# Layer 0 of a two-layer diffusion backbone: six output blocks kept split, early first weights, low parts of the norms on VectorE

## The chip, the cores and the metric

The kernel runs on one core of one Trainium2 chip. The metric is the device time of one execution in microseconds (us); the time before is the median of three runs. TensorE is the matrix engine, VectorE (DVE in the rows) and ScalarE (ACT) work on elements, POOL is GpSimd, and SP is the queue from which nearly all DMAs are issued.

## The reference, cut to what matters

There are 512 latent tokens and 256 context tokens of width 1024, and two layers. The change lies mostly in layer 0:

```
x, h: 512 latent tokens, 256 context tokens
layer 0:
  y = concat(gated_linear_heads(u), windowed_attention(u)) @ w_out      # mixer
  x = layer_norm(ALPHA * x + gate * y)                                  # first norm
  x = layer_norm(ALPHA * x + gate5 * squared_relu(mod(x) @ w1) @ w2)    # MLP, second norm
  the same for h with its own modulation
layer 1: other mixers, then the same pair of norm and MLP, latent tokens only
```

The modulation vectors (gate, shift, scale) are products of two conditioning vectors with large matrices.

## The kernel before, in words

**Numbers.** Dense products are made in fp32r, a format of fewer bits. Each operand is split in two: a high part, cast by ScalarE, and a low part, which is what the cast left, subtracted by VectorE (`split`, L323 to L326). A product is three matmuls, high x high (L346), high weight x low activation (L348) and low weight x high activation (L350), in that order for each of eight slices k of 128 rows. Activations lie transposed, 128 features by tokens, latents first (512 columns), then context (256).

**Weights** (`weights`, L328). A block of 128 x 1024 is loaded into a raw buffer by a DMA from SP and then split into a high and a low buffer. Without `keep`, the buffers come from the pool `wp`, which rotates them: in layer 0 after the mixer five raw, two high and two low. With `keep` each block has high and low buffers of its own. Load and split are given a priority 1000 places ahead of their place in the code (`prio`, PW). The framework turns the code into one ordered list per engine: what has its operands and buffers ready and the lowest priority number goes next, by a modelled time. On the chip every engine, and SP's queue, runs its list in order, and a tile that takes the place of an older one waits until that one's last reader is done.

**Layer 0's mixer** (`mixer0`). The gated-linear heads (`gla`) and the eight attention heads (`gqa`, scores one head ahead of `attend`) are interleaved as generators; when `gla` has ended, attention runs on alone. A head ends with two logarithms and an exponential on ScalarE (L832 to L834), two products on VectorE (L839, L840), and for every second head the split of the result into activation slice 4 + h/2 (L325, L326). The pool `m1` holds the gated-linear part's work tiles, `mb` those of attention; `m0` what both need.

**Output projection** (`project`). For two token parts (512 latent, 256 context columns), for eight output blocks d: get weight block d, 24 matmuls into one of six PSUM banks, add to the residual z (L1032), add z up for the norm (L1034, L1036). Layer 0 keeps no block: the eight blocks are loaded and split for the latents and again for the context. After a part, the generator `norm` of that part becomes `fill`, and two of its steps are taken after each block of the next part.

**Norm** (`norm`). Mean by a matmul with ones (L1066), subtraction on VectorE (L1076), squares on ScalarE (L1078), their mean by matmuls (L1074), reciprocal root on ScalarE (L1085, L1086). Then for each k: product on VectorE (L1090), the high part of the next activation on ScalarE (L1103), the same unrounded on VectorE into `lnu` (L1104), and their difference, the low part, on POOL (L1106). ScalarE then scales z (L1112). This happens twice in layer 0 for both parts (512 and 256 columns) and once in layer 1 for two halves of 256.

**MLP** (`mlp`). Four hidden blocks at a time. For the first four, `first` goes over the parts; on the latents the blocks are taken in the pairs (0, 1) and (2, 3), with one step of the context part's norm after every second k; on the context one by one. `up` and `down` follow for the rest. Between them `step` takes a row of the modulation matrices of later use (`ada_chunk`): it is loaded into a raw buffer of the same five and reduced by VectorE (L394).

Of the kernel before, what the change touches and what calls it, by code (L numbers as in the profile page):

```python
# [16 lines left out]
P = 128  # L17
D = 1024
KT = D // P
# [25 lines left out]
PL = 50  # L45
PZL = 300
# [189 lines left out]
def blocks(*ws):  # L236

    return [tuple(w[d].rearrange("p k m -> p (k m)") for w in ws) for d in range(KT)]
# [21 lines left out]
class Build:  # L260
# [67 lines left out]
    def weights(self, src, n=1024, keep=None, lead=PW):  # L328

        raw = self.wp.tile([P, 1024], F32, tag="wraw", name="wraw")  # L330
        pool, bufs, d = (self.wp, 2, '') if keep is None else (keep[0], 1, keep[1])
        hi = pool.tile([P, 1024], F32R, tag=f"whi{d}", name="whi", bufs=bufs)
        lo = pool.tile([P, 1024], F32R, tag=f"wlo{d}", name="wlo", bufs=bufs)
        with self.prio(-lead):
            src = src if isinstance(src, tuple) else (src,)
            m = n // len(src)
            for i, s in enumerate(src):
                self.nc.sync.dma_start(raw[:, i * m:i * m + m], s)
            self.split(raw[:, :n], hi[:, :n], lo[:, :n])
        return hi[:, :n], lo[:, :n]  # L340
# [372 lines left out]
    def gqa(self, m0, mx_, queries, KS, K2, vg, hi, lo):  # L713
# [73 lines left out]
        def attend(h):  # L787
# [41 lines left out]
            mm(oc[:, 0:256], sl, Q2[sink, CX], start=False, stop=True)  # L829
            r, ro = HALF[par], HALF[1 - par]  # L830
# [21 lines left out]
        for h in range(8):  # L852
            a = scores(h + 1) if h < 7 else iter(())
            for _ in attend(h):
                next(a, None)
                yield
            for _ in a:
                yield

    def mixer0(self):  # L860
# [3 lines left out]
        with tc.tile_pool(name="m0", bufs=1, side="right", reuse_waits="tile") as m0, ExitStack() as m0_, \  # L864
# [119 lines left out]
            with tc.tile_pool(name="mb", bufs=1, reuse_waits="tile") as mb:  # L984
                self.zerob = mb.tile([P, P], BF16, name="zerob")
                nc.gpsimd.memset(self.zerob, 0.0)
                self.identb = mb.tile([P, P], BF16, name="identb")
                nc.gpsimd.tensor_copy(self.identb, ident)
                self.maskb = [mb.tile([P, P], BF16, name=f"maskb{i}") for i in range(2)]
                mt = m1.tile([P, 2 * P], F32, tag="Dt", name="mt", bufs=4)  # L990
                nc.sync.dma_start(mt, self.a['band'])
                for i in range(2):
                    nc.gpsimd.tensor_copy(self.maskb[i], mt[:, i * P:(i + 1) * P])
                self.gla_setup(mb)

# [12 lines left out]
                for _ in att:  # L1008
                    pass
            self.psum(**PF)  # L1010
        return mhi, mlo


    def project(self, ws, hi, lo, z, g, l, parts, sums, norm, keep=None, kept=(), lead=PW):
# [6 lines left out]
        for i, (t0, m) in enumerate(parts):  # L1021
            sl = slice(t0, t0 + m)
            for d in range(KT):
                wh, wl = kept.get(d) or self.weights(ws[d], keep=keep and (keep, d), lead=lead)
                if keep:
                    kept[d] = wh, wl
# [21 lines left out]
    def norm(self, pool, z, sums, l, i, w, part, act=None, nxt=None, out=None, spill=None):  # L1048
# [39 lines left out]
        for k in range(KT):  # L1088
# [12 lines left out]
            else:  # L1101
# [3 lines left out]
                eng = nc.gpsimd  # L1105
                eng.tensor_tensor(lo[:, k, sl], u, hi[:, k, sl].bitcast(F32), op=ALU.subtract)  # L1106
# [11 lines left out]
    def mlp(self, pool, l, hi, lo, z, parts, fill, step=lambda: None, first_parts=None):  # L1118
# [14 lines left out]
        def first():  # L1133
# [3 lines left out]
            for i, (t0, m) in enumerate(first_parts or parts):  # L1137
                sl = slice(t0, t0 + m)
                for pair in ((0, 1), (2, 3)) if i == 0 else ((0,), (1,), (2,), (3,)):
# [51 lines left out]
    def layer0(self):  # L1191
        nc, tc = self.nc, self.tc
        hi, lo = self.mixer0()
        self.wopen(5)
        self.fq = self.es2.enter_context(tc.tile_pool(name="fq", bufs=1, side="right", reuse_waits="tile"))
        fq = self.fq
        with tc.tile_pool(name="zp", bufs=1, side="right", reuse_waits="tile") as zp, \
# [25 lines left out]
            fill = self.project(blocks(self.a['w0_o']), ks(hi), ks(lo), z, 2, 0, PARTS, sums, norm(0, (0, 4, 3)))  # L1223
            hs = self.mlp(f0, 0, *act, z, PARTS, fill, step)
            for _ in gen:
                pass
            fill = self.project(blocks(self.a['w2_0'][6], self.a['w2_0'][7]), *hs, z, 5, 0, PARTS, sums, norm(1, (1, 1, 0), self.zd))

            self.shift_setup(fq)
# [7 lines left out]
            for _ in fill:  # L1237
                pass
        return act
# [778 lines left out]
    def wopen(self, bufs=3):  # L2018
# [42 lines left out]
```

## Time and profile before

| | us |
|---|---|
| three runs | 2063.58, 2064.16, 2066.43 |
| median | 2064.16 |
| profiled execution, its own time | 2064.74 |
| its span, first to last instruction | 2063.0 |

The median is what the comparison goes by; the rows are of the profiled execution. In a row of the timeline the first number is the start in us from the span's beginning, the second the time until the group's last end; [x <-y] is the idle time of the engine just before it, and what ended it. PE is TensorE's matmul stream, PEld its weight loads. Matmul rows overlap, so their starts say more than their lengths.

### The profile page before, as it was taken

What the parts mean: (1) busy time and instruction counts of PE and PEld (TensorE: products, weight loads), DVE (VectorE), ACT (ScalarE), POOL (GpSimd) and SP (SyncE); (2) the same over time, 40 slices, a digit from 0 to 9 for tenths busy, and PEclk for the clock granted to TensorE, in tenths of its full rate; (3) what the DMA queues carried; (4) which work ended last, traced back from release to release, by engine and by line L of the source; (5) the groups of instructions that cost most, each with busy time, mean ns of one, the idle gap of its engine ahead of it and who ended that gap; (6) DMA issues with size and microseconds to landing.
All of it is one profiled execution on the core that took longest, in us unless ns stands there. A gap on an engine that the chain in (4) does not pass through costs nothing.

```text
span 2063.0 us, 35320 instructions
## 1 busy us (share of the span) xinstructions
PE 1937.1 (94%) x14244; PEld 1613.2 (78%) x14244; DVE 1311.3 (64%) x2341; ACT 962.4 (47%) x1840; POOL 295.9 (14%) x503
## 2 busy tenths in 40 slices
PE   8999798999999999999989999988888999999998
PEld 7887666677788888888877876757776888888887
DVE  8785999638897556534485455467876665444454
ACT  5536777535522222222255656766665654333332
POOL 0003566202100000000021020024231020000001
PEclk9998899999999999999999999998999999999999
DMA  8650000053454555313243100000001513323241
GB/s 297 213 167 11 1 1 1 1 204 112 132 167 134 156 163 148 112 53 92 82 140 139 47 1 19 16 8 3 3 3 34 167 42 94 108 92 91 89 137 42
DMA packets 67047, 181.67 MB, mean 88 GB/s; under 512 B 7490, under 2 KB 12354, under 8 KB 66756
## 3 DMA queue, kind: packets, MB, share of 16 engines
q1 hardware_dynamic: 66884, 179.42, 27.9%
q8 instruction: 112, 1.84, 0.4%
q14 instruction: 51, 0.42, 0.1%
HBM read 172.83 MB, written 5.51 MB: 86 GB/s over the span
## 4 chain that ended last, share of the span: by engine, by line
PE 68%; DVE 15%; ACT 8%; DMA 4%; issue 4%; POOL 1%; SPq 0%; DVEq 0%; ACTq 0%; POOLq 0%
PE mm L350 17%; PE mm L348 17%; PE mm L346 17%; DMA araw<-in_ada_r_dram 3%; PE var L1074 2%; DVE wlo L326 2%; PE mo L1492 1%; PE ms L1466 1%; PE gab L1624 1%; DVE aprod L394 1%; PE gx L1740 1%; DVE z L1090 1%; DVE lq L621 1%; DVE araw L394 1%; PE go L795 1%
## 5 line engine op out<-in xcount | busy, mean ns | idle before, releaser
L325 ACT CAST whi<-wraw 128x1024 fp32r<-128x1024 f32 (+2 forms) x253 | 221.8, 880 | 625.6 <-PE mm L348 538.2
L346 PE MATMUL mm<-acthi,whi 128*128 128x512 f32 (+1 forms) x1464 | 446.2, 351 | 10.8 <-ACT whi L325 10.1
L350 PE MATMUL mm<-acthi,wlo 128*128 128x512 f32 (+1 forms) x1464 | 440.4, 347 | 9.2 <-DVE wlo L326 9.2
L348 PE MATMUL mm<-actlo,whi 128*128 128x512 f32 (+1 forms) x1464 | 442.7, 348 | 1.6 <-POOL actlo L1106 1.5
L326 DVE TENSOR_TENSOR wlo<-wraw,whi 128x1024 fp32r<-128x1024 f32 (+2 forms) x253 | 258.3, 1024 | 207.0 <-ACT whi L325 200.5
L346 PEld LDWEIGHTS mm<-acthi,whi 128*128 128x128 f32 x1464 | 252.1, 192 | 49.5 <-ACT whi L325 12.5
L350 PEld LDWEIGHTS mm<-acthi,wlo 128*128 128x128 f32 x1464 | 252.0, 192 | 48.7 <-DVE wlo L326 12.8
L348 PEld LDWEIGHTS mm<-actlo,whi 128*128 128x128 f32 x1464 | 252.3, 192 | 40.6 <-issue 3.9
L350 PE MATMUL mm<-hh,wlo 128*128 128x512 f32 (+1 forms) x832 | 253.1, 342 | 3.6 <-DVE wlo L326 3.6
L346 PE MATMUL mm<-hh,whi 128*128 128x512 f32 (+1 forms) x832 | 255.2, 344 | 0.2 <-ACT hh L325 0.2
L348 PE MATMUL mm<-hl,whi 128*128 128x512 f32 (+1 forms) x832 | 253.2, 342 | 0.1
L1106 POOL TENSOR_TENSOR actlo<-lnu,acthi 128x256 fp32r<-128x256 f32 (+1 forms) x48 | 59.9, 1263 | 715.2 <-DVE lnu L1104 635.2
L350 PEld LDWEIGHTS mm<-hh,wlo 128*128 128x128 f32 x832 | 143.5, 189 | 23.5 <-DVE wlo L326 4.2
L348 PEld LDWEIGHTS mm<-hl,whi 128*128 128x128 f32 x832 | 144.0, 189 | 20.2 <-issue 0.7
L346 PEld LDWEIGHTS mm<-hh,whi 128*128 128x128 f32 x832 | 143.3, 189 | 19.9 <-issue 1.0
L1178 DVE SCALAR_TENSOR_TENSOR z<-mm,mod,z 128x512 f32<-128x512 f32 (+1 forms) x144 | 94.1, 660 | 98.3 <-PE mm L350 98.1
L394 DVE SCALAR_TENSOR_TENSOR araw<-araw,scb 128x1024 f32<-128x1024 f32 x80 | 97.9, 1223 | 54.8 <-DMA araw<-in_ada_r_dram 53.9
L325 ACT CAST hh<-relu 128x512 fp32r<-128x512 f32 (+1 forms) x100 | 50.6, 535 | 79.7 <-DVE relu L1130 79.7
L1032 DVE SCALAR_TENSOR_TENSOR z<-mm,mod,z 128x256 f32<-128x256 f32 (+1 forms) x64 | 35.0, 549 | 76.7 <-PE mm L350 75.7
L619 POOL TENSOR_TENSOR lk<-kd,Dt 64x128 f32<-64x128 f32 x144 | 75.5, 524 | 35.0 <-ACT Dt L601 13.5
L326 DVE TENSOR_TENSOR hl<-relu,hh 128x512 fp32r<-128x512 f32 (+1 forms) x100 | 56.2, 588 | 26.5 <-ACT hh L325 26.2
L394 DVE SCALAR_TENSOR_TENSOR aprod<-araw,scb 128x1024 bf16<-128x1024 f32 x48 | 58.6, 1222 | 22.1 <-DMA araw<-in_ada_r_dram 21.8
(462 smaller groups left out, 3215.3 us busy)
## 6 DMA issues: line engine op xcount, KB each, us to landing
araw<-in_ada_r_dram SPq DMA_DIRECT2D x80, 512.0 KB, 3.8
wraw<-in_w_dram SPq DMA_DIRECT2D x72, 512.0 KB, 3.6
wraw<-in_w_dram SPq DMA_DIRECT2D x144, 256.0 KB, 2.7
wraw<-in_w_s_dram SPq DMA_DIRECT2D x31, 512.0 KB, 4.0
wraw<-in_w_o_dram SPq DMA_DIRECT2D x22, 512.0 KB, 3.6
scraw<-in_ada_sc_dram SPq DMA_DIRECT2D x8, 512.0 KB, 7.5
shraw<-in_ada_sh_dram SPq DMA_DIRECT2D x8, 512.0 KB, 6.1
x<-in_xT_dram SPq DMA_DIRECT2D x8, 384.0 KB, 5.6
```

The costliest lines, as they stand in the source:

```text
L325: self.nc.scalar.copy(hi, raw)
L326: (eng or self.nc.vector).tensor_tensor(lo, raw, hi.bitcast(F32), op=ALU.subtract)
L346: mm(o, whi, ahi[:, sl], start=first, stop=False)
L348: mm(o, whi, alo[:, sl], start=False, stop=False)
L350: mm(o, wlo, ahi[:, sl], start=False, stop=last)
L394: self.nc.vector.scalar_tensor_tensor(pr, raw, 1.0, self.scb[:, w], op0=ALU.mult, op1=ALU.mult, accum_out=out(w))
L619: nc.gpsimd.tensor_tensor(K[r, :, x], kk[r, :, x], d[r, :, x], op=ALU.mult)
L621: nc.vector.tensor_tensor(Q[r, :, y], qq[r, :, y], d[r, :, y], op=ALU.mult)
L1032: nc.vector.scalar_tensor_tensor(zs, o, self.mod[:, l, self.wh(i, parts), g, d:d + 1], zs, op0=ALU.mult, op1=ALU.add)
L1074: nc.tensor.matmul(var, self.c('o1024', 0, P), sq, start=(k == 0), stop=(k == KT - 1))
L1106: eng.tensor_tensor(lo[:, k, sl], u, hi[:, k, sl].bitcast(F32), op=ALU.subtract)
L1178: nc.vector.scalar_tensor_tensor(z[:, d, sl], o, self.mod[:, l, self.wh(i, parts), 5, d:d + 1], z[:, d, sl], op0=ALU.mult, op1=ALU.add)
```

## The change

It has six parts. Six blocks (`KO`, d = 2 to 7) of layer 0's output projection are kept split, in a pool `fk` whose place the MLP's hidden tiles (`fh`) and then the tiles of the shift (`fs`) take over later. The pool of weights is opened inside the mixer, when the last head has only its closing elementwise work left and `m1` has been closed, and blocks 0 and 1 are asked for there (`first`). That pool has four raw, three high and two low buffers instead of five, two and two. The low parts in `norm` go from POOL to VectorE, in all norms that feed another product. The second pair of the MLP's first latent part becomes two single blocks in layer 0. The zero, identity and mask tiles of attention come after the clearing of the second set of level tiles in the code, at a priority 100 places ahead.

```diff
-        hi = pool.tile([P, 1024], F32R, tag=f"whi{d}", name="whi", bufs=bufs)
+        hi = pool.tile([P, 1024], F32R, tag=f"whi{d}", name="whi", bufs=bufs if keep else self.wb)
...
             mm(oc[:, 0:256], sl, Q2[sink, CX], start=False, stop=True)
+            if h == 7:
+                yield True
...
-            for _ in attend(h):
+            for last in attend(h):
                 next(a, None)
-                yield
+                yield last
...
-                self.zerob = mb.tile([P, P], BF16, name="zerob")
-                nc.gpsimd.memset(self.zerob, 0.0)
...
                 self.gla_setup(mb)
+                with self.prio(-100):
+                    self.zerob = mb.tile([P, P], BF16, name="zerob")
+                    nc.gpsimd.memset(self.zerob, 0.0)
...
-                for _ in att:
-                    pass
+                for last in att:
+                    if last:
+                        break
+            m0_.close()
+            self.wopen(4, 3)
+            ws = blocks(self.a['w0_o'])
+            first = {d: self.weights(ws[d]) for d in range(2)}
+            for _ in att:
+                pass
             self.psum(**PF)
-        return mhi, mlo
+        return mhi, mlo, first
...
-                wh, wl = kept.get(d) or self.weights(ws[d], keep=keep and (keep, d), lead=lead)
-                if keep:
+                k = keep and d in keeps
+                wh, wl = kept.get(d) or first.pop(d, None) or self.weights(ws[d], keep=k and (keep, d) or None, lead=lead)
+                if k:
                     kept[d] = wh, wl
...
-                eng = nc.gpsimd
-                eng.tensor_tensor(lo[:, k, sl], u, hi[:, k, sl].bitcast(F32), op=ALU.subtract)
+                nc.vector.tensor_tensor(lo[:, k, sl], u, hi[:, k, sl].bitcast(F32), op=ALU.subtract)
...
-                for pair in ((0, 1), (2, 3)) if i == 0 else ((0,), (1,), (2,), (3,)):
+                for pair in ((0, 1), (2,), (3,)) if i == 0 and l == 0 else ((0, 1), (2, 3)) if i == 0 else ((0,), (1,), (2,), (3,)):
...
-        hi, lo = self.mixer0()
-        self.wopen(5)
+        hi, lo, first = self.mixer0()
...
-            fill = self.project(blocks(self.a['w0_o']), ks(hi), ks(lo), z, 2, 0, PARTS, sums, norm(0, (0, 4, 3)))
-            hs = self.mlp(f0, 0, *act, z, PARTS, fill, step)
+            with tc.tile_pool(name="fk", bufs=1, reuse_waits="tile") as fk:
+                fill = self.project(blocks(self.a['w0_o']), ks(hi), ks(lo), z, 2, 0, PARTS, sums, norm(0, (0, 4, 3)), fk,
+                                    first=first, keeps=KO)
+            fh_ = ExitStack()
+            fh = fh_.enter_context(tc.tile_pool(name="fh", bufs=1, reuse_waits="tile"))
+            hs = self.mlp(fh, 0, *act, z, PARTS, fill, step)
...
+            fh_.close()
+
+            fs_ = ExitStack()
+            f0 = fs_.enter_context(tc.tile_pool(name="fs", bufs=1, reuse_waits="tile"))
```

## Rows read from the trace of the kernel before

**Rows 1.** The page, part 1: busy time, share of the span, instructions.

```profile
PE 1937.1 (94%) x14244; PEld 1613.2 (78%) x14244; DVE 1311.3 (64%) x2341; ACT 962.4 (47%) x1840; POOL 295.9 (14%) x503
```

**Rows 2.** Windows: length; busy PE, PEld, DVE, ACT, POOL; PEclk; DMA share; GB/s.

```profile
400.00:420.00 20.00, 18.92 (x76) 11.83 (x75) 4.94 (x14) 9.58 (x19) 0.21 (x4) 0.83 0.08 26
420.00:430.00 10.00, 4.98 (x12) 3.45 (x13) 5.24 (x18) 4.04 (x6) 0.00 (x0) 0.74 0.82 290
```

**Rows 3.** Timeline 415 to 432: start, us, engine, line, operation [idle before, releaser].

```profile
415.44 12.19 SPq L338 DMA_DIRECT2D wraw<-in_w_o_dram  x7
...
419.93 0.38 PE L829 MATMUL goc<-q,sel 3*128 3x256 f32 x1
...
422.35 0.93 ACT L325 CAST acthi<-ga 128x512 fp32r<-128x512 f32 x2 [0.76 <-DVE ga L839]
...
424.27 0.50 PE L346 MATMUL mm<-acthi,whi 128*128 128x512 f32 x1 [3.97 <-ACT whi L325]
...
426.19 0.80 PE L350 MATMUL mm<-acthi,wlo 128*128 128x512 f32 x1 [1.05 <-DVE wlo L326]
...
431.48 0.43 PE L350 MATMUL mm<-acthi,wlo 128*128 128x512 f32 x1
```

**Rows 4.** Timeline of ScalarE: two neighbouring high-part casts of the output projection.

```profile
460.99 1.06 ACT L325 CAST whi<-wraw 128x1024 fp32r<-128x1024 f32 x1 [4.38 <-PE mm L348]
...
466.43 1.06 ACT L325 CAST whi<-wraw 128x1024 fp32r<-128x1024 f32 x1 [4.38 <-PE mm L348]
```

**Rows 5.** Timeline of TensorE, from the projection's context part to the MLP's steady part.

```profile
471.89 0.28 PE L346 MATMUL mm<-acthi,whi 128*128 128x256 f32 x1
...
474.76 1.02 PE L1066 MATMUL mu<-sums,col 128*128 128x512 f32 x2
...
478.49 1.88 PE L1074 MATMUL var<-lnsq,col 128*128 128x512 f32 x4
...
496.62 0.58 PE L350 MATMUL mm<-acthi,wlo 128*128 128x256 f32 x1 [2.16 <-DVE wlo L326]
...
555.44 0.52 PE L346 MATMUL mm<-acthi,whi 128*128 128x512 f32 x2
```

**Rows 6.** Window, latent norm's second half: length; busy DVE; PEclk; DMA share; GB/s.

```profile
489.90:518.00 28.10, 28.10 (x36) 0.94 0.30 96
```

**Rows 7.** Timeline of VectorE, and POOL's first row, in the same stretch.

```profile
424.92 2.36 DVE L326 TENSOR_TENSOR wlo<-wraw,whi 128x1024 fp32r<-128x1024 f32 x2
...
491.12 0.54 DVE L1104 TENSOR_SCALAR lnu<-z,gb 128x512 f32<-128x512 f32 x1
...
491.83 1.30 POOL L1106 TENSOR_TENSOR actlo<-lnu,acthi 128x512 fp32r<-128x512 f32 x1 [73.95 <-DVE lnu L1104]
...
491.96 1.44 DVE L1104 TENSOR_SCALAR lnu<-z,gb 128x512 f32<-128x512 f32 x1
...
526.86 1.29 DVE L326 TENSOR_TENSOR hl<-relu,hh 128x512 fp32r<-128x512 f32 x2
```

**Rows 8.** Timeline of TensorE in layer 0's second norm: first, fifth and last gap.

```profile
1064.05 0.38 PE L350 MATMUL mm<-hh,wlo 128*128 128x256 f32 x1 [2.16 <-DVE wlo L326]
...
1081.35 0.50 PE L348 MATMUL mm<-actlo,whi 128*128 128x512 f32 x1 [0.89 <-POOL actlo L1106]
...
1106.70 0.50 PE L350 MATMUL mm<-acthi,wlo 128*128 128x512 f32 x1 [0.65 <-DVE wlo L326]
```

**Rows 9.** Timeline of SP's queue and TensorE in the MLP's steady part.

```profile
736.64 0.33 SPq L408 DMA_DIRECT2D araw<-in_ada_r_dram  x1
...
741.59 0.33 SPq L408 DMA_DIRECT2D araw<-in_ada_r_dram  x1
...
758.90 0.62 PE L350 MATMUL mm<-acthi,wlo 128*128 128x512 f32 x2 [0.20 <-DVE wlo L326]
```

**Rows 10.** Timeline of POOL and TensorE at the start of the GLA stage.

```profile
203.17 0.21 POOL L986 MEMSET zerob<- 128x128 bf16 x1
...
205.15 0.28 PE L645 MATMUL base<-zerob 128*128 128x256 bf16 x1
```

More of the change, by code (lines that the diff above doesn't have):

```diff
@@ L45 @@
 PL = 50
+KO = 2, 3, 4, 5, 6, 7
 PZL = 300
@@ L984, in mixer0 @@
             with tc.tile_pool(name="mb", bufs=1, reuse_waits="tile") as mb:
-                self.zerob = mb.tile([P, P], BF16, name="zerob")
-                nc.gpsimd.memset(self.zerob, 0.0)
[L987 to L993, printed above, removed]
-                self.gla_setup(mb)
+                self.gla_setup(mb)
+                with self.prio(-100):
+                    self.zerob = mb.tile([P, P], BF16, name="zerob")
+                    nc.gpsimd.memset(self.zerob, 0.0)
+                    self.identb = mb.tile([P, P], BF16, name="identb")
+                    nc.gpsimd.tensor_copy(self.identb, ident)
+                    self.maskb = [mb.tile([P, P], BF16, name=f"maskb{i}") for i in range(2)]
+                    mt = m1.tile([P, 2 * P], F32, tag="Dt", name="mt", bufs=4)
+                    nc.sync.dma_start(mt, self.a['band'])
+                    for i in range(2):
+                        nc.gpsimd.tensor_copy(self.maskb[i], mt[:, i * P:(i + 1) * P])
                 def queries(i):
@@ L1007, in mixer0, with project @@
                         next(att, None)
-                for _ in att:
-                    pass
+                for last in att:
[7 more added lines that the diff above has]
+                pass
             self.psum(**PF)
-        return mhi, mlo
-    def project(self, ws, hi, lo, z, g, l, parts, sums, norm, keep=None, kept=(), lead=PW):
+        return mhi, mlo, first
+    def project(self, ws, hi, lo, z, g, l, parts, sums, norm, keep=None, kept=(), lead=PW, first={},
+                keeps=range(KT)):
         nc = self.nc
@@ L1238, in layer0 @@
                 pass
+            fs_.close()
         return act
@@ L2016, in close, with wopen @@
         self.es.close()
-    def wopen(self, bufs=3):
+    def wopen(self, bufs=3, wb=2):
+        self.wb = wb
         self.wes = ExitStack()
```

## The prediction

> **What bounds the kernel now.** I read the page's busy shares first: TensorE is busy 94% of the span and VectorE 64% [rows 1], so the time is TensorE's own work plus the places where TensorE waits. What matters is where those places are. The windows by stage came next [rows 2]. Around the hand-over from layer 0's attention to its output projection TensorE is busy 4.98 of 10 us, at a mean granted clock of 0.74, while ScalarE is about half used in the 20 us before. The timeline of that hand-over [rows 3] shows why. The last attention matmul starts at 419.93 and lasts 0.38; the projection's first matmul starts at 424.27, after 3.97 us of waiting for the first weight block's high part; the third waits again, for the low part, until 426.19. The weight loads are issued from 415.44 on. The thirteen matmuls from 426.19 to 431.48 start 0.44 us apart, the lower of the clock's two levels (1.2 GHz); later a block of 24 takes 5.44 [rows 4], 0.227 apiece, the upper level (2.4 GHz).
>
> Second place: from the first 256-column matmul of the projection (471.89) to the first matmul of the MLP's steady part (555.44) TensorE stops again and again, mostly for a low part made on VectorE, 2.16 us at 496.62 for instance [rows 5]. In that stretch VectorE is busy all of 28.10 us [rows 6]. Third place: the same pattern in the second norm of layer 0, seven gaps from 1064.05 to 1106.70 that make 6.8 us together, one of them behind the low part that POOL writes [rows 8].
>
> **The parts, step by step.**
>
> *Hand-over.* Blocks 0 and 1 are loaded and split before the last head ends, so TensorE can go on at 420.31 (419.93 + 0.38 [rows 3]). Its first 21 matmuls need k = 0 to 6, which exist; k = 7 is written by the casts of 422.35 and the subtractions right behind them, and TensorE gets there at 420.31 + 21 x 0.227 = 425.1. A block takes 5.44 us at the full clock (distance of the casts at 460.99 and 466.43 [rows 4]), eight take 43.5; before, 471.89 - 420.31 = 51.6 [rows 3, 5]. With no idle gap there the clock should not fall. So up to 8.1 us go. Against this, two casts of 1.06 [rows 4] and two subtractions of 1.2 [rows 7] now stand among the last heads' work, and SP's and ScalarE's queues are in order: an exponential behind such a cast is late by up to 1.06 (two: 2.1), by more if the cast has been queued ahead of data that isn't there. VectorE has room (4.94 busy of 20 [rows 2]). Between 0 and 8.1, I take 1.0 of cost: **-7.1 us**. Other loads aren't passed: SP has nothing else to issue there, and the z loads come later, as now, behind the weights; the six PSUM banks of the products cover their lateness.
>
> *Kept blocks, three high buffers, single second pair, low parts on VectorE: 471.89 to 555.44, 83.55 us.* TensorE's own work in it, at the full clock: eight projection blocks of 2.87 (471.89 to 474.76 [rows 5]) make 23.0; four MLP blocks of 24 x 0.23 = 5.5 make 22.0; four of 2.87 make 11.5; the latent norm's sums take 0.9 plus four groups of 1.7 (1.88 less the overlap [rows 5]), the context norm's about half, together 12.3. Sum 68.8, so 14.7 us are lost now. What VectorE had to do in its full 28.10 us [rows 6] shrinks: six blocks are no longer split a second time (6 x 1.2 = 7.2 of VectorE, 6 x 1.06 = 6.4 of ScalarE, and six loads of 512 KB). The low parts cost 8 x 0.62 more (the equal form, 1.29 for two [rows 7]) = 5.0. But POOL's part was not free: beside it lnu took 1.44 instead of 0.54 [rows 7], 0.9 for each of eight, 7.2. Net 28.1 - 7.2 + 5.0 - 7.2 = 18.7, so VectorE ends some 9 us sooner and the MLP's first matmul waits for nothing. With three high parts the next cast doesn't wait for TensorE, and blocks 2 and 3 one by one let the context norm advance 12 steps instead of 8 in the first part, so its results are there when the MLP's 256-column blocks want them. What is late next: the low part of block 2, which has only two buffers and follows the pair (0.3 to 1.2 us), and the context sums (about 1). I leave 3.2 of the 14.7: **-11.5 us**; bounds -5 and -14.7.
>
> What POOL costs VectorE: the row shows 0.9 us lost per POOL subtraction that itself takes 1.30 [rows 7]. The Trainium skill, SBUF — State Buffer, section "Who interferes with whom", says that such a pair excludes each other for the whole instruction. By that each would cost VectorE up to 1.30, and the relief would be 10.4 instead of 7.2; as an estimate, the next part would then gain some 3 us more and the forecast come to 2040.5. The measured 0.9 stands.
>
> *Second norm of layer 0.* No weights are kept here; only POOL's share goes and the third high buffer comes. VectorE: 8 x (0.62 - 0.9) = -2.2 for the latents, about the same again for POOL's own latency, which TensorE waited for at 1081.35 [rows 8]. Of 6.8 us I take **-2.8**; bounds +2 (VectorE no freer) and -6.8. Layer 1's 16 low parts (256 columns): at nothing, 1 us either way, since VectorE pays and is repaid alike.
>
> *Four raw buffers instead of five*, shared by weights and modulation rows during the MLP. There SP issues the next row when the one before has been used, 736.64 and 741.59, and TensorE waits 0.20 us at 758.90 [rows 9]. One buffer less shortens the lead of the weights; the third high part gives back a little. Between 0 and +4: **+0.4**.
>
> *Order of the mask tiles and the clearing in POOL's queue.* The zero tile is written at 203.17, its first reader starts at 205.15 without a wait [rows 10]: 1.8 us of cover, so nothing. If the ten clearings came first, up to 2 us. The pools that now share memory (kept blocks, then the hidden layer, then the shift) follow each other on TensorE: nothing.
>
> Sum: -7.1 - 11.5 - 2.8 + 0.4 = -21.0. The profiled execution took 2064.74 (span 2063.0), 0.6 above the median 2064.16: 2043.7 against it, **2043.5** rounded towards the median.
>
> **Rivals.**
> 1. *The hand-over keeps its wait in another place.* The early buffers lie where the gated-linear part's tiles were; if they come free late, or the casts stand in front of the last heads' exponentials with their data still on the way, the 8.1 us are paid there. For it: ScalarE's order is fixed, attention is a chain over it. Against: ScalarE is half idle [rows 2]. Then 2050.6. Chance 0.10.
> 2. *VectorE becomes the bound.* If the long rows beside POOL are not POOL's doing but something that stays, VectorE's stretch shrinks only from 28.1 to 25.9, the first gain falls to about 5 and the second norm loses 2.5: 2043.5 + 6.5 + 5.3 = 2055.3. Against it: the same forms are short when POOL is quiet [rows 7]. Chance 0.14.
> 3. *Slower: the row chain with four buffers.* One modulation row circulates in 4.95 us (736.64 to 741.59 [rows 9]); a step of the MLP's second half takes 12 x (0.227 + 0.12) = 4.2, so a group of eight falls behind by 8 x 0.79 = 6.3 us, which the weights asked for ahead cover. With one buffer less the lead is 3 x 4.2 = 12.5; the lag and one more circuit want 6.3 + 4.95 = 11.3. If it is a little worse, TensorE waits up to 6.3 in each of the four groups that carry rows: +25, that is 2068.7. It decides where the lead falls under the lag. For it: 0.20 us of waiting already. Chance 0.07.
> 4. *Something in the order changes elsewhere* (GLA stage, layer 1), or the stalls of the second place return in other spots: near 2060. Chance 0.07.
>
> **How the numbers follow.** The forecast has 0.62. About 0.2% (4 us) is what a measurement of this kernel can tell from no change. Forecast and rivals 1 and 2 are all faster by more, 0.86, plus 0.02 of rival 4: 0.88; same 0.05 (rest of rival 4); slower 0.07. Low end: all bounds on the good side give -30.6; 2036 takes most of it. High end: past rival 2, 2057. Outside remain rivals 3 and 4 and the tails, under 0.2.
>
> **What would show it.** Right: the matmul after the last attention matmul follows within 1 us and the projection's first part takes about 44 us at clock 1.00; no POOL row at the norm's low part, lnu 0.54 throughout; sixteen output-projection splits become ten; from the first 256-column matmul to the MLP's steady part about 72 us; gaps of the second norm near 4. Wrong: an exponential of the last heads waiting behind a high-part cast; VectorE still full for 25 us; TensorE waits for low parts between 556 and 860 in groups of eight.

## The result and the profile after

The changed kernel takes 2040.17 us (median of 4 runs, 2037.43 to 2043.07) against 2063.87 for the kernel before in the same comparison: ratio 0.989, 95% interval 0.9872 to 0.9908. The forecast was 2043.5 in a range of 2036 to 2057. The profiled execution took 2037.43 (span 2035.5), 27.3 less than the one before; it is the fastest of the four, so the stages below add up to more than the medians' 23.7. That the total came out near the forecast is in part luck: one term of the sum fell short by 5.2 us and three others brought 12.8 more than forecast.

The timeline of the hand-over after the change, one fence for TensorE, ScalarE, VectorE and SyncE; it answers to [rows 3] and [rows 2]. Columns: start, duration, engine, line, operation, idle time before it and what ended it.

```profile
402.87 28.25 SPq L339 DMA_DIRECT2D wraw<-in_w_o_dram  x9
...
419.42 0.38 PE L830 MATMUL goc<-q,sel 3*128 3x256 f32 x1
423.77 0.50 PE L347 MATMUL mm<-acthi,whi 128*128 128x512 f32 x1 [3.96 <-ACT whi L326]
425.03 0.80 PE L351 MATMUL mm<-acthi,wlo 128*128 128x512 f32 x1 [0.47 <-DVE wlo L327]
...
421.85 0.92 ACT L326 CAST acthi<-ga 128x512 fp32r<-128x512 f32 x2 [0.76 <-DVE ga L842]
422.68 3.88 ACT L326 CAST whi<-wraw 128x1024 fp32r<-128x1024 f32 x4
...
423.75 4.63 DVE L327 TENSOR_TENSOR wlo<-wraw,whi 128x1024 fp32r<-128x1024 f32 x4
```

The first weight load is issued 12.57 us earlier (402.87 for 415.44), the second 5.44 (414.93 for 420.37), and TensorE still waits 3.96 us for the first high part, as before (3.97). ScalarE casts it right behind the last head's closing casts, although the data had lain there for long.

Windows after the change: the hand-over, VectorE's stretch in the first norm, and the second norm with the next stage's input. Columns: stretch, its length, busy time (instructions) of PE, PEld, DVE, ACT, POOL, then the granted clock. The last row is the third window in the kernel before.

```profile
420.00:430.00 10.00, 5.76 (x18) 4.33 (x19) 7.31 (x11) 6.82 (x9) 0.00 (x0) 0.83 0.40 123
487.50:504.60 17.10, 17.10 (x127) 16.37 (x127) 17.10 (x36) 11.96 (x16) 0.00 (x0) 1.00 0.00 1
1034.00:1114.00 80.00, 80.00 (x431) 66.82 (x430) 54.82 (x100) 50.26 (x77) 0.80 (x14) 1.00 0.44 149
```

```profile
1034.00:1114.00 80.00, 73.24 (x382) 59.22 (x380) 63.86 (x94) 46.40 (x69) 22.59 (x26) 0.98 0.40 122
```

VectorE's full stretch shrank from 28.10 us [rows 6] to 17.10, and TensorE is busy through all of it. (The 28.10 also hold two modulation rows of 1.21 us. From the norm's first z to the fourth addition to the context sums VectorE took 25.30 us before, with five splits of weights among them, and 16.68 now, with none.) Over the whole stretch of 83.55 us TensorE's idle time fell from 8.75 us to 0.33 and its busy time from 74.80 to 68.87, at a granted clock of 1.00 instead of 0.94. In the second norm TensorE is busy all of the 80 us, and GpSimd's 22.59 us beside VectorE are gone (the changed kernel is 16 us ahead there, so the two windows don't hold quite the same work). Of the gaps of [rows 5] one of 0.19 us is left in the first norm's stretch, and none of those of [rows 8].

**Where the time went, by stage.** Each stage is the distance of two starts in TensorE's timeline. *Hand-over*: the last head's second value product to the first 256-column block of the projection. *First norm*: from there to the MLP's steady part. *Second norm*: its 256-column part to the end of the next stage's input. *Layer-1 norm*: first mean to the first 512-column block. *RWKV/MLA*: from the second norm's end to the group norm; no experiment edits it, TensorE runs the same matmuls there in the same order in all 14 profiles, and its spread shows what one profile is worth. Medians come from different comparisons, in which the kernel before took 2062.86 to 2067.37; the ratio, taken within each comparison, is what compares.

| kernel | hand-over | first norm | second norm | layer-1 norm | RWKV/MLA | span | median | ratio to before, 95% |
|---|---|---|---|---|---|---|---|---|
| before | 53.02 | 83.55 | 129.47 | 62.83 | 438.67 | 2063.0 | 2063.87 | |
| after | 51.12 | 69.20 | 119.12 | 60.42 | 440.47 | 2035.5 | 2040.17 | 0.989 [0.9872, 0.9908] |
| e1 first weights not early | 51.08 | 69.18 | 118.84 | 60.43 | 440.28 | 2033.1 | 2040.19 | 0.9888 [0.9866, 0.991] |
| e2 no kept blocks | 51.00 | 74.14 | 118.83 | 60.43 | 442.50 | 2042.5 | 2044.67 | 0.9906 [0.9886, 0.9926] |
| e3 low parts on GpSimd | 51.08 | 80.26 | 126.08 | 63.19 | 442.42 | 2058.8 | 2058.75 | 0.9968 [0.9952, 0.9983] |
| e4 two high buffers | 51.05 | 73.04 | 119.30 | 60.40 | 445.04 | 2044.0 | 2045.05 | 0.9902 [0.9881, 0.9923] |
| e5 hidden tiles as before | 52.31 | 72.61 | 119.37 | 60.42 | 440.84 | 2041.1 | 2042.99 | 0.9904 [0.9881, 0.9927] |
| e6 first split on GpSimd | 49.98 | 69.18 | 118.84 | 60.42 | 440.89 | 2035.3 | 2038.23 | 0.9874 [0.9852, 0.9896] |
| e7 layer 1: three high | 52.24 | 69.19 | 118.86 | 58.74 | 441.19 | 2036.3 | 2038.33 | 0.9874 [0.985, 0.9898] |
| e8 before + low parts on VectorE | 52.72 | 75.31 | 119.35 | 60.40 | 439.15 | 2045.3 | 2046.49 | 0.9913 [0.9892, 0.9934] |
| e9 e6 into kept tiles | 45.03 | 69.09 | 119.14 | 60.43 | 443.04 | 2034.5 | 2033.73 | 0.9844 [0.9823, 0.9865] |
| e10 e7, single blocks | 51.08 | 69.20 | 119.15 | 57.22 | 446.34 | 2040.2 | 2040.42 | 0.9868 [0.9846, 0.9889] |
| e11 second pair back | 52.33 | 76.02 | 118.83 | 60.42 | 442.69 | 2045.0 | 2045.39 | 0.99 [0.9874, 0.9926] |
| e12 e9 and e10 | 45.01 | 69.08 | 118.86 | 57.21 | 443.52 | 2036.8 | 2031.27 | 0.9828 [0.9801, 0.9854] |

Before to after: -1.90, -14.35, -10.35, -2.41, and +1.80 in RWKV/MLA; the MLP between the norms took 0.63 more (483.88, 484.51). In RWKV/MLA the longest profiles have the lower granted clock (0.93 in e4, 0.94 in e10, 0.95 in before and after). Still, the two kernels without the change's buffers, before and e8, have the two shortest times of the 14 (438.67, 439.15), so a small cost of the change there isn't excluded.

### The profile page after: what moved, and what is told of

Read it like the earlier page. It is cut to its first block, busy times and chain, and to the rows that moved or that the text cites. A ratio compares the mean times of both kernels' runs of the same rounds, so it can differ in the third digit from the quotient of the medians.

```text
span 2035.5 us, 35292 instructions
## 1 busy us (share of the span) xinstructions
PE 1924.9 (95%) x14244; PEld 1605.9 (79%) x14244; DVE 1301.0 (64%) x2383; ACT 956.2 (47%) x1834; POOL 238.2 (12%) x455
## 4 chain that ended last, share of the span: by engine, by line
PE 74%; DVE 11%; ACT 8%; issue 3%; DMA 3%; POOL 1%; SPq 0%; ACTq 0%; DVEq 0%; POOLq 0%
PE mm L349 18%; PE mm L347 18%; PE mm L351 18%; PE var L1087 2%; DMA araw<-in_ada_r_dram 2%; PE ms L1485 1%; PE mo L1511 1%; PE gab L1643 1%; DVE aprod L395 1%; PE gx L1759 1%; PE go L796 1%; DVE wlo L327 1%; PE st L1525 1%; DVE lq L622 1%; ACT GT L1656 1%
## 5 line engine op out<-in xcount | busy, mean ns | idle before, releaser
L326 ACT CAST whi<-wraw 128x1024 fp32r<-128x1024 f32 (+2 forms) x247 | 215.2, 876 | 610.4 <-PE mm L349 530.2
L347 PE MATMUL mm<-acthi,whi 128*128 128x512 f32 (+1 forms) x1464 | 440.1, 348 | 8.7 <-ACT whi L326 7.9
L351 PE MATMUL mm<-acthi,wlo 128*128 128x512 f32 (+1 forms) x1464 | 435.8, 344 | 0.9 <-DVE wlo L327 0.8
L327 DVE TENSOR_TENSOR wlo<-wraw,whi 128x1024 fp32r<-128x1024 f32 (+2 forms) x247 | 246.9, 1003 | 212.3 <-PE mm L351 101.3
```

The source lines that it names most:

```text
L326: self.nc.scalar.copy(hi, raw)
L327: (eng or self.nc.vector).tensor_tensor(lo, raw, hi.bitcast(F32), op=ALU.subtract)
L347: mm(o, whi, ahi[:, sl], start=first, stop=False)
L351: mm(o, wlo, ahi[:, sl], start=False, stop=last)
```

## The experiments

All start from the changed kernel unless the text says otherwise.

**e1: no early request.**

```
-            first = {d: self.weights(ws[d]) for d in range(2)}
+            first = {}
```

> The changed kernel, but its first two output blocks are no longer asked for ahead of the last head's end; everything else stays. Theory (the early loads land, but ScalarE's list holds the first high-part casts behind the last head's closing casts, so that only the transfer's own lateness was removed): from the end of the last head's matmuls to the first 256-column block of the projection 51.5 us instead of 49.68, whole time up by 1.5 to 2.5 us (ratio to the changed kernel 1.001). Rival (the early loads do more, among other things by the clock they leave behind): up by 5 us or more. Rival (the early loads cost in the GLA stage what they give at the hand-over): the end of the last head comes 0.5 to 1 us earlier and the whole time is within 1 us.

The hand-over took 51.08 (51.12), the median 2040.19 (2040.17): no theory held. The timeline of this run, SyncE and TensorE: the first load was issued at 399.15, and the first product waited the same 3.96 us.

```profile
399.15 32.23 SPq L339 DMA_DIRECT2D wraw<-in_w_o_dram  x10
...
421.69 0.50 PE L347 MATMUL mm<-acthi,whi 128*128 128x512 f32 x1 [3.96 <-ACT whi L326]
```

Compared engine by engine, the two programs hold the same instructions in the same order with the same waits: the scheduler pulls the weights forward either way. So the run is a repeat of the changed kernel, and the written early request does nothing. That its profile's span is 2.4 us shorter, 2.6 of it before the attention stage begins, is what a repeat gives.

**e5: what does bring the loads early** (on top of e2, below).

```
-            hs = self.mlp(fh, 0, *act, z, PARTS, fill, step)
+            hs = self.mlp(f0, 0, *act, z, PARTS, fill, step)
```

> The run without kept blocks, and in addition the MLP's hidden tiles go back into the buffer pool that is opened ahead of the projection, where the kernel before had them; the lines that ask for the first weights early stay in. Theory (the weights come early because the space under their buffers is free earlier, not because of where the request stands in the program; the run that left the request out had its first weights issued at 399.15, no later than with it): the first output block's load is issued only at 413 to 416 us, as before the change, and from the start of the last head's second value product to the first 256-column block it takes 52.5 to 53.1 us as before (53.02) instead of 51.0; whole time 1.5 to 2 us above the run without kept blocks (2044.67). Rival (the written request brings them early): issue at 399 to 405 us, 51.0 us, the same time as the run without kept blocks.

The timeline of this run, SyncE and TensorE:

```profile
412.69 12.19 SPq L339 DMA_DIRECT2D wraw<-in_w_o_dram  x5
...
421.53 0.79 PE L347 MATMUL mm<-acthi,whi 128*128 128x512 f32 x1 [3.96 <-ACT whi L326]
```

The loads are late again (412.69), with the early request still in the program. It is the place of the hidden tiles that decides when the space under the weights is free, as the theory said. Its times missed: 52.31 for 52.5 to 53.1, and a whole time of 2042.99, below e2's 2044.67 instead of above it. What the early loads are worth is another matter: e7 and e11, with early loads, took 52.24 and 52.33. What differs is how long the products come 0.43 us apart, the clock's lower level: for 3.6 us from the first one after the change (to 427.33), for 6.1 in e7 (425.17 to 431.29), 5.5 in e5. So of the change's -1.90 only 0.6 is shorter waiting for the low part (1.05 [rows 3], 0.47 now). The rest goes with the shorter time at the lower clock. Of the eight profiles with early loads and ScalarE's splits, six (after, e1 to e4, e10) took 51.00 to 51.12 and two (e7, e11) 52.24 and 52.33; the three with late loads (before, e5, e8) took 52.31 to 53.02. Early loads may make the short one more likely; that isn't shown.

**e6: the first splits away from ScalarE's list.**

```
-            first = {d: self.weights(ws[d]) for d in range(2)}
+            first = {d: self.weights(ws[d], eng=nc.gpsimd) for d in range(2)}
...
-        self.nc.scalar.copy(hi, raw)
+        (cast or self.nc.scalar.copy)(hi, raw)
```

> The changed kernel, but the first two output blocks are split on GpSimd (cast and subtraction), which does nothing else from 400 to 430 us. Theory (at the hand-over TensorE waits for casts that stand in ScalarE's list behind the last head's closing casts): TensorE begins the projection within 0.5 us of the last head's end instead of 3.96 us later, the wait of 0.47 us goes too, and the low clock after it is shorter or gone; from the start of the last head's second value product to the first 256-column block 44.5 to 47 us instead of 51.1, whole time down by 4 to 6.5 us (ratio to before 0.986). Rival (GpSimd's splits are slow, or wait for the space of the split tiles until the head has ended): the wait turns into one for GpSimd, 50 to 53 us, whole time from 1 us down to 2 us up.

The timeline of this run, GpSimd and TensorE:

```profile
420.63 1.04 POOL L326 CAST whi<-wraw 128x1024 fp32r<-128x1024 f32 x1 [30.21 <-PE goc L830]
421.75 2.37 POOL L327 TENSOR_TENSOR wlo<-wraw,whi 128x1024 fp32r<-128x1024 f32 x1
...
421.72 0.50 PE L347 MATMUL mm<-acthi,whi 128*128 128x512 f32 x1 [1.30 <-POOL whi L326]
424.17 0.50 PE L351 MATMUL mm<-acthi,wlo 128*128 128x512 f32 x1 [1.72 <-POOL wlo L327]
```

The rival's mechanism held: 1.1 us gained (49.98, just outside its 50 to 53), and the whole time can't be told from the changed kernel's. An idle engine with the data at hand casts only at 420.63, when the head's last product (goc) has ended: the split tiles lie where that product still reads. ScalarE's order hid a second wait, for space.

**e9: GpSimd, and other space.** Blocks 0 and 1 become kept blocks, whose tiles lie elsewhere; 2 and 3 are loaded again instead.

```
-KO = 2, 3, 4, 5, 6, 7
+KO = 0, 1, 4, 5, 6, 7
...
-            first = {d: self.weights(ws[d]) for d in range(2)}
+            first = {}
...
+                wh, wl = kept.get(d) or self.weights(..., eng=self.nc.gpsimd if first and d < 2 and i == 0 else None)
```

> The changed kernel, but the first two output blocks are split on GpSimd, and into the tiles of kept blocks (blocks 0, 1 and 4 to 7 are kept, 2 and 3 are loaded again), which lie elsewhere than the turning buffers. In the run with GpSimd alone its first cast began only at 420.63 us, released by the last head's last product, although its data had been there for long. Theory (two things stand in line at the hand-over: ScalarE's list, and behind it the space of the split tiles, which the last head still reads): with both gone TensorE begins the projection within 0.5 us of the head's end (0.0 to 0.5 instead of 3.96), and from the start of the last head's second value product to the first 256-column block it takes 45 to 47.5 us instead of 51.1; whole time down by 4 to 6 us. Rival (the place of the first low-part tile is still read late, or TensorE waits for the last head's activations in the first block instead): a wait of 1.5 to 4 us remains within the first block, 49 to 51 us, whole time down by 0 to 2 us.

The timeline of this run, GpSimd and TensorE, and behind it the window of the hand-over:

```profile
409.47 1.04 POOL L326 CAST whi<-wraw 128x1024 fp32r<-128x1024 f32 x1 [17.19 <-DMA wraw<-in_w_o_dram]
410.58 2.36 POOL L327 TENSOR_TENSOR wlo<-wraw,whi 128x1024 fp32r<-128x1024 f32 x1
...
420.25 0.38 PE L830 MATMUL goc<-q,sel 3*128 3x256 f32 x1
420.57 0.50 PE L347 MATMUL mm<-acthi,whi 128*128 128x512 f32 x1
```

```profile
420.00:430.00 10.00, 10.00 (x45) 8.00 (x44) 6.85 (x10) 6.61 (x9) 3.10 (x2) 1.00 0.72 247
```

The cast now runs 11 us earlier, TensorE goes on without a wait, its clock stays at the upper level (1.00 for 0.83), and the hand-over takes 45.03. The median is 6.4 below the changed kernel's, and the intervals of the two ratios don't meet. The hand-over is 8.0 us shorter than in the kernel before (53.02): this is what the change's early weights were to bring. The run changes the engine and the space at once. ScalarE casting into these other tiles wasn't tried, and since the lists are ordered by a modelled time at which operands and space are ready, ScalarE's late place may itself come from the space. That the engine had to change too is not shown.

**e3: the norms' low parts back on GpSimd.**

```
-                nc.vector.tensor_tensor(lo[:, k, sl], u, hi[:, k, sl].bitcast(F32), op=ALU.subtract)
+                nc.gpsimd.tensor_tensor(lo[:, k, sl], u, hi[:, k, sl].bitcast(F32), op=ALU.subtract)
```

> The changed kernel, but the norms' low parts go back to GpSimd in every norm. Theory (GpSimd's subtractions stretch VectorE's lnu from 0.54 to 1.44 us, so the move relieved VectorE although it gave it 16 more operations): in the stretch of layer 0's first norm 3 to 6 us more than 69.20, in the second norm's stage (second norm's 256-column part to the end of the next projection's input, 119.12 us) 4 to 8 more, with gaps released by VectorE's low parts; whole time up by 7 to 14 us. Rival (with kept blocks and three high buffers VectorE has slack, and where the low parts run is indifferent): each stage within 1 us, whole time within 2 us.

First norm +11.06, second +6.96, layer 1 +2.77, whole time +18.6 by the medians: the theory's direction, and more than it gave in the first norm (3 to 6) and in the whole time (7 to 14). VectorE's timeline in the first norm of this run (in the changed kernel lnu takes 0.54 throughout), and then TensorE's in both norms:

```profile
489.13 0.54 DVE L1117 TENSOR_SCALAR lnu<-z,gb 128x512 f32<-128x512 f32 x1
489.59 0.48 DVE L1045 SCALAR_TENSOR_TENSOR z<-mm,mod,z 128x256 f32<-128x256 f32 x1
489.99 1.45 DVE L1117 TENSOR_SCALAR lnu<-z,gb 128x512 f32<-128x512 f32 x1
...
496.61 1.51 DVE L1049 TENSOR_TENSOR sums<-sums,z 128x256 f32<-128x256 f32 x1
```

```profile
507.87 1.22 PE L1079 MATMUL mu<-sums,col 128*128 128x256 f32 x2 [4.24 <-DVE sums L1049]
...
1072.24 0.50 PE L349 MATMUL mm<-actlo,whi 128*128 128x512 f32 x1 [1.58 <-POOL actlo L1118]
```

The context norm's sums came 4.24 us late, and TensorE waited for GpSimd itself.

**e8: the kernel before, with the low parts on VectorE alone.**

```
-                eng = nc.gpsimd
+                eng = nc.vector
```

> The kernel before the change, with one part of it alone: the norms' low parts run on VectorE instead of GpSimd. Theory (this is the part that relieved VectorE in both norms of layer 0: putting the low parts back on GpSimd cost 11.06 us in the first norm's stretch and 6.96 in the second's stage): the first norm's stretch 76 to 79 us instead of 83.55, from the second norm's 256-column part to the end of the next projection's input 122 to 124 us instead of 129.5; whole time 10 to 14 us below before (ratio 0.994). Rival (16 more operations on VectorE pay only where kept blocks and a third high buffer have made room on it; that was the other rival of the prediction, VectorE as the bound): stretch 82 to 86 us, ratio 0.997 to 1.001.

-8.24, -10.12 and -2.43 us, and 16.4 in the whole time (2062.86 to 2046.49), each more than the theory gave: this one word is most of the change, and it pays without kept blocks or a third buffer. Its ratio of 0.9913 has an interval that overlaps the whole change's. The second norm's gain is nearly all its own. VectorE's work of 25.30 us in the kernel before, from the norm's first z to the fourth addition to the context sums, is done in 22.46 with eight low parts more. TensorE gained more than these 2.84 us: in the first norm's stretch its idle time fell from 8.75 us to 3.86 and its busy time from 74.80 to 71.45, at a clock of 1.00 instead of 0.94. The windows of that stretch, in this run and in the kernel before:

```profile
490.00:512.70 22.70, 22.53 (x151) 20.53 (x150) 22.46 (x39) 17.14 (x22) 0.00 (x0) 1.00 0.40 122
```

```profile
489.90:515.20 25.30, 20.77 (x134) 18.66 (x133) 25.30 (x30) 16.77 (x21) 13.57 (x8) 0.93 0.33 104
```

Its MLP took 484.51 with five raw buffers, so the +0.63 is not the fourth buffer's price.

**e2, e4, e11: the other three parts of the first norm's stretch, each undone.**

```
e2: -KO = 2, 3, 4, 5, 6, 7
    +KO = ()
e4: -            self.wopen(4, 3)
    +            self.wopen(4, 2)
e11:-... ((0, 1), (2,), (3,)) if i == 0 and l == 0 else ((0, 1), (2, 3)) if i == 0 else ...
    +... ((0, 1), (2, 3)) if i == 0 else ...
```

> The changed kernel, but no output block is kept split: all eight are loaded and split a second time for the 256 columns. Theory (VectorE is the bound of that stretch, and six splits of 2.31 us less there are the larger part of its gain): the stretch from the first 256-column block to the MLP's steady start takes 78 to 83 us instead of 69.20, with gaps released by VectorE's low parts at the block starts; whole time up by 9 to 14 us. Rival (the low parts that moved from GpSimd to VectorE had been what slowed VectorE's norm, and the kept blocks matter little): 70 to 72 us, whole time up by at most 3 us.

> The changed kernel with two high-part buffers instead of three in layer 0. Theory (VectorE's relief removed the second norm's gaps; the third high buffer only lets ScalarE cast ahead): the second norm's stage 119 to 121 us instead of 119.12, the first norm's stretch 69 to 71; whole time up by 0 to 3 us. Rival (the third buffer is what removed those gaps, since with two the next block's cast waits for the end of the block before): short gaps of 0.4 to 1.2 us released by ScalarE at the starts of blocks, as in layer 1's norm, some 16 of them: 6 to 10 us more.

> The changed kernel, but in layer 0 the third and fourth block of the feed-forward's first part run as a pair again. Theory (VectorE's relief and three buffers do the work there, and the order of two blocks is worth little): the first norm's stretch 69 to 71 us instead of 69.20, whole time within 1.5 us. Rival (with the pair both splits are due at once behind the norm's last activations, and a gap of 1 us or more brings the half clock with it, as in the run with two high buffers): 72 to 74 us, whole time up by 3 to 5 us.

The first norm's stretch grew by 4.94, 3.84 and 6.82. For e2 (4.5 in the whole time) the theory gave 9 to 14 and the rival at most 3, so both miss. For e4 the third buffer did nothing in the second norm, as the theory said, and something in the first, which it did not say; the whole time (+4.9) lies between theory and rival. For e11 the rival held, and the stretch (76.02) went past its 72 to 74. Nearly all of it arises in the last piece, the MLP's first 256 columns: 12.54 us after the change, 16.95, 16.31 and 19.33 in these runs. TensorE's timeline in that piece of e11, then the windows of it in e11 and e4:

```profile
531.92 0.39 PE L349 MATMUL mm<-actlo,whi 128*128 128x256 f32 x1 [0.78 <-DVE actlo L1118]
533.49 0.50 PE L347 MATMUL mm<-acthi,whi 128*128 128x256 f32 x2 [0.83 <-ACT acthi L1116]
...
537.79 0.38 PE L349 MATMUL mm<-actlo,whi 128*128 128x256 f32 x1 [1.81 <-DVE actlo L1118]
539.31 0.58 PE L347 MATMUL mm<-acthi,whi 128*128 128x256 f32 x1 [0.78 <-ACT whi L326]
```

```profile
524.00:546.40 22.40, 17.70 (x112) 15.86 (x111) 20.38 (x42) 16.17 (x30) 0.00 (x0) 0.92 0.38 120
```

```profile
524.36:540.67 16.31, 14.03 (x97) 13.20 (x96) 14.80 (x28) 10.13 (x18) 0.00 (x0) 0.90 0.42 134
```

In e11 the context norm's last variance group starts 50.36 us after the first 256-column block (520.71), after the change 47.61 (517.09): with the pair the norm gets fewer of its steps in, and its low parts are late. In e4 the gaps make 2.28 us and the piece is 3.77 longer; the clock, 0.90 instead of 1.00, is most of the rest. The clock need not fall: e2 and e5 have the same three gaps there (0.38, 0.28 and 1.02), e2 at a clock of 0.90 with a piece of 16.95, e5 at 1.00 with 15.44. The three costs add up to 15.6, and with e3's to 26.7, where the whole change gave 14.35: the parts overlap, and any one of them left out leaves gaps there.

**e7, e10: layer 1.** Three high buffers there (paid with one of five lnu buffers); e10 also takes blocks 2 and 3 one by one.

```
-        self.open()
+        self.open(3, 3)
...
e10: -... if i == 0 and l == 0 else ((0, 1), (2, 3)) if i == 0 else ...
     +... if i == 0 else ...
```

> The changed kernel, and layer 1's feed-forward stage also gets three high-part buffers (paid for with one of the five lnu buffers). Theory (the eight gaps of 0.28 to 1.17 us in layer 1's norm, 4.7 us in all, are released by casts that wait for one of two high buffers; layer 0 had the same kind of gain from its third): from the stage's first mean to its first 512-column block 56 to 58 us instead of 60.42; whole time down by 2.5 to 4.5 us. Rival (ScalarE is late there by its own work, or VectorE's low parts take the place): 59.5 to 60.5 us, whole time within 1 us.

> The run with three high-part buffers in layer 1, and in addition layer 1's first part of the feed-forward takes its third and fourth block one by one instead of as a pair, as the change does in layer 0. Theory (the pair needs both casts at once; in the run with three buffers alone 4.6 us of gaps remained, four of them released by ScalarE's casts and activations): from the stage's first mean to its first 512-column block 56.5 to 58 us instead of 58.74 (and 60.42 in the changed kernel); whole time 0.5 to 2 us below the run with three buffers. Rival (the norm's activations, not the weights, come last there, and a single block asks for them twice as fast as a pair): 59 to 61 us, no gain or up to 2 us more than with the pair.

The stage shrinks by 1.68 and 3.20. The second is as expected; the first is less: some waits for high parts became waits for VectorE's low parts. TensorE's timeline of e7:

```profile
1661.48 0.39 PE L351 MATMUL mm<-acthi,wlo 128*128 128x256 f32 x1 [0.84 <-DVE wlo L327]
...
1677.31 0.50 PE L347 MATMUL mm<-acthi,whi 128*128 128x256 f32 x2 [0.87 <-ACT acthi L1116]
```

In the whole time neither can be told from the changed kernel, and e10's median lies above e7's instead of below it: RWKV/MLA ahead of the stage took 446.34 in e10's profile.

**e12: e9 and e10 together.**

> Both gains together: the first two output blocks split on GpSimd into kept tiles, and layer 1's feed-forward with three high-part buffers and its third and fourth block one by one. Theory (the two are in stages 1200 us apart and add): from the start of the last head's second value product to the first 256-column block 45.0 us (51.12 in the changed kernel), layer 1's norm 57.2 us (60.42), together 9.3 us; whole time 2029 to 2033 us, ratio to before 0.983. Rival (layer 1's part gives nothing in the whole time, as its run with single blocks came to 2040.42 although its stage was 3.2 us shorter, because the stage before it varies by more): 2033 to 2036 us, the same as the run with the hand-over alone (2033.73).

Both stages came out as alone (45.01 and 57.21). The median of 2031.27 and the ratio of 0.9828, both as the theory had them, are the lowest of all. The interval doesn't meet the changed kernel's, but against e9 (2033.73) the intervals overlap: that layer 1's part shows in the whole time stays open.

## Why the prediction was right, and where it was not

The sum's terms missed by +5.2, -2.9, -7.6 and -2.4 us (hand-over, first norm, second norm, layer 1), so the forecast's place inside the measured spread is partly luck.

*Hand-over, -7.1:* -1.9, of which shorter waiting explains 0.6. The step that failed is its first sentence, "Blocks 0 and 1 are loaded and split before the last head ends". They were loaded and not split. Rival 1 had the event (the buffers come free late) but put the price at queued exponentials; the wait simply stayed where it was, behind ScalarE's list and behind that the space (e6). With both changed e9 came 8.0 below the kernel before (8.1 was the step's upper bound), so the step's size was right, and its condition was not.

*First norm, -11.5:* -14.35. The mechanism was right, VectorE's load above all: 9.4 us less worked out, 8.6 seen (25.30 to 16.68). Some details were off. Only three of the six second splits stood in the 28.10 us of [rows 6] (495.35, 497.55, 503.01); the two at 506.91 and 511.53 are the MLP's first, which after the change come at 512.11 and 513.25. And the sums of the two norms, 0.9 + 4 x 1.7 and half of it, make 11.6 and not 12.3. The weights of the parts were off too: the working gave the kept blocks 7.2 us of VectorE and the low parts a net 2.2, but without kept blocks the stretch grew by 4.94 us (e2) and with the low parts on GpSimd by 11.06 (e3). The 3.2 kept back for "what is late next" was the error: 0.19 us of gaps remained. The step on blocks 2 and 3 one by one is borne out by e11.

*Second norm, -2.8:* -10.35, past its own bound of -6.8. The bound took TensorE's listed gaps [rows 8] for all that could be lost. All the stage's idle time went (7.00 us to 0.00), and 3.35 us more of TensorE's busy time (122.47 to 119.12). The clock had fallen as well, as a window of the kernel before shows; the 0.17 that is missing there makes 1.7 us in 10:

```profile
1080.00:1090.00 10.00, 7.98 (x28) 5.91 (x27) 7.60 (x16) 4.39 (x9) 1.30 (x1) 0.83 0.53 158
```

In the first norm the working took the stretch's length less TensorE's own work at the full clock, which contains such losses; in the second it counted gaps alone. And it took a relief of 2.2 us on VectorE, with GpSimd's own delay, for 2.8 us of TensorE's time. In e8 that relief alone left 0.17 us of the 7.00: the rows that GpSimd had lengthened were low parts of weights for which TensorE waited, or stood ahead of them. Here are VectorE and GpSimd in the kernel before, in the first norm:

```profile
493.66 1.77 DVE L1090 TENSOR_TENSOR z<-z,lnr 128x512 f32<-128x512 f32 x1
...
497.55 2.30 DVE L326 TENSOR_TENSOR wlo<-wraw,whi 128x1024 fp32r<-128x1024 f32 x1
...
506.91 1.21 DVE L326 TENSOR_TENSOR wlo<-wraw,whi 128x1024 fp32r<-128x1024 f32 x1
507.14 2.15 POOL L1106 TENSOR_TENSOR actlo<-lnu,acthi 128x512 fp32r<-128x512 f32 x1 [1.75 <-DVE lnu L1104]
508.05 1.52 DVE L1104 TENSOR_SCALAR lnu<-z,gb 128x512 f32<-128x512 f32 x1
...
509.71 1.61 POOL L1106 TENSOR_TENSOR actlo<-lnu,acthi 128x512 fp32r<-128x512 f32 x1 [0.42 <-DVE lnu L1104]
510.09 0.47 DVE L1032 SCALAR_TENSOR_TENSOR z<-mm,mod,z 128x256 f32<-128x256 f32 x1
510.48 1.12 DVE L1104 TENSOR_SCALAR lnu<-z,gb 128x512 f32<-128x512 f32 x1
...
512.66 1.51 DVE L1036 TENSOR_TENSOR sums<-sums,z 128x256 f32<-128x256 f32 x1
```

The weights' subtraction takes 1.21 when GpSimd is quiet (495.35), so 1.09 is lost at 497.55. Eight such rows between 491.96 and 512.66 lose 7.8 us, 0.98 for each of GpSimd's eight operations; the prediction's 0.9, which it charged in both norms, was the right size.

The Trainium skill, SBUF — State Buffer, section "Who interferes with whom", says that a VectorE operation with two SBUF inputs contends with GpSimd's reads, and one with a single SBUF input does not outside the modes that use both ports. The rows agree: the projection's z, one input from PSUM, stays at 0.47 inside GpSimd's operation (510.09), while sums goes from 0.42 to 1.51. lnu is stretched too, with one SBUF input; by that section it would have to run in such a mode, which no run here shows. Its rule that whoever issues first holds the ports and the other is blocked for the whole instruction fits as well. GpSimd's operation at 507.14 ends at 509.29, and lnu, begun at 508.05, ends 0.28 later; the one at 509.71 ends at 511.32, and lnu again 0.28 later (511.60). VectorE loses less than the 1.30 of an undisturbed GpSimd operation because its row starts when part of that is over. GpSimd loses in turn: the one at 507.14 begins while wlo runs (506.91 to 508.12) and takes 2.15.

*Layer 1, 0 within 1:* -2.41 in its norm; there too VectorE was not "repaid alike" but freed (e3: 63.19, e8: 60.40). *Raw buffers, +0.4:* +0.63 in the MLP, but not from the buffers (e8), so no run supports rival 3. Four against five raw buffers by themselves weren't tried. *Mask order, 0:* the attention stage took 213.69 (213.72); not tried by itself. *Rival 2* fell with e8: the long rows were GpSimd's doing.

## What to carry to other kernels

Where GpSimd and VectorE work in the same stretch, price a GpSimd operation by what it adds to VectorE's rows and not only by its own engine: moving 48 subtractions, 16 in each of three stages, onto the fuller engine gained 20.8 us over these stages (e8). A load that lands earlier is worth nothing until the next operation has its turn in its engine's list and the space for its output; look at both before writing an early request, and compare the programs' order to see whether the request changes anything. The last gaps in a stretch of short matmuls cost more than their length: 4.70 us of gaps made the piece 6.79 longer in e11, 2.28 made it 3.77 longer in e4. The lower clock can follow them and can stay away: 1.78 us of gaps made the piece 4.41 longer in e2, where the clock fell, and 2.90 in e5, where it did not.

## What was not expected of the hardware

A cast of 128x1024 takes 1.04 us on GpSimd, as long as on ScalarE (1.05), while the subtraction of the same size takes 2.36 there and 1.21 on VectorE. And the same program, profiled twice, began its attention stage at 204.67 and at 202.10 us; in RWKV/MLA, which no experiment edits, the profiles ranged from 438.67 to 446.34 with the same matmuls in the same order, the longest at a clock of 0.94, the shortest at 0.95. A gain of 3 us shows in a stage's timeline and not in the whole time.
